# Seventy-two of eighty early expert blocks as unsplit fp32 products, and twenty-eight of their results held in SBUF

## The chip, the core and the metric

The kernel runs on one core of one Trainium2 chip. The metric is the device time of one execution in microseconds (us). The engines are TensorE (PE in the rows, PEld for its weight loads), VectorE (DVE), ScalarE (ACT), GpSimd (POOL) and SyncE (SP, which only issues copies here).

## What is computed

One decoder layer over 512 tokens of width 1024 in fp32. Three groups of attention heads and an output projection come first. Then comes a feed-forward part in which each token has 8 heads, and each head retrieves 16 of 16384 one-neuron experts:

```python
    cand = (v1[..., :, None] + v2[..., None, :])            # scores of two half keys
    top_s, pos = lax.top_k(cand, PEER_TOPK)
    expert = jnp.take_along_axis(cand_idx, pos, axis=-1)
    gate = jax.nn.softmax(top_s, axis=-1)
    a = jnp.einsum('cd,ced->ce', x_c, u[e_c])               # h . u of each chosen expert
    w = jax.nn.gelu(a, approximate=False) * g_c
    return jnp.einsum('ce,ced->cd', w, v[e_c])              # sum of w * v
```

The attention is outside of this study. All of the change lies in the expert part.

## The kernel before, in words

**Two ways through the experts.** For the first 128 tokens (chunk `GC`) the kernel gathers the rows that were chosen: 128 gathers of rows of `u`, each followed by a dot product on VectorE (`dot`, L494), a gelu, and 128 gathers of rows of `v`, each added up on VectorE (L505). For the next 64 tokens it gathers rows of `u` alone, 64 times, with the same `dot`. For the last 320 tokens (`TD`) it computes the product of the tokens with **all** rows of `u`, in 128 blocks of 128 experts (`a_block`). For all 384 tokens outside `GC` the product with `v` runs over all 128 blocks too (`w_block`), with a weight that is zero where an expert wasn't chosen.

**A block's first product.** `u_parts` (L529) loads 512 KB of `uT` into one of three buffers `flat`. Where the block is split, ScalarE writes a rounded copy `hi` (L91), VectorE the remainder `lo` (L92), both into `yT`, and the buffer `flat` is free again. `a_block` (L539) then issues three products for each of eight slices (`mm3`, L100 to L102), 24 in all, on operands of type fp32r. Where the block is whole (L527), nothing is split. `flat` itself is the weight of eight plain fp32 products with `hF` (L544), and stays occupied until they are done. `hF` is a sum that GpSimd makes once (L608). A gelu on ScalarE (L551) moves the result out of PSUM into `ag`, of which two can be under way in PSUM (tag `t`).

**Early and late blocks.** Blocks 0 to 79 (`NSP`) are early: their first products run while routing and scatter are still going on. The result of most is written to DRAM (`ad`, L658) and read back before the second product (`agr`, L684). The last `KEEP` of them stay in SBUF instead (`kept`, L548), in a pool `kp` that is opened at L651. Blocks 80 to 127 are late. Their first products alternate with the second products of all 128 blocks.

**Routing and scatter.** VectorE picks experts and gates (`top16`, `route`). Then `scatter` (L615) makes the table of weights: for every four tokens a one-hot tile `o1` (L621), four gated one-hot tiles `o2` (L625), four products on TensorE (L628) and a copy on ScalarE (L629) into `stage`. Eight such units fill one `stage`, which goes to DRAM (`gd`, L633). There are 96 units. Those of the 64 tokens (`iX`) need the dots of these tokens (L642 to L648). The second products need the finished table (`gt`, L688) and the PSUM banks that scatter has used.

**What sets the order.** The program is recorded, and a scheduler then fixes one order of instructions for each engine. On the chip every engine works through its own list. Gathers go through four buffers `row`, one queue of GpSimd. All other copies are issued by SP in one list. Rows of `u` for `GC` are one step for each early block (L659 to L661), and the rest follows where the scheduler puts it. The pool `rp` with routing's tiles was open to the end.

The numbers that choose which blocks are whole and which are kept:

```python
KEEP = 8
WHOLE = 48
    def whole(b):
        return WHOLE <= b < NSP and b % 2 == 1
```

Of the kernel before, what the change touches and what calls it, by code (L numbers as in the profile page):

```python
# [37 lines left out]
NSP = 80  # L38
# [6 lines left out]
SCB = 4  # L45
EM = 4
GR = 1.0
KEEP = 8
WHOLE = 48
HX = P // 2  # L50
DX = DC[0]
T0 = DX * P + HX
# [8 lines left out]
def layer_kernel(ctx, tc, x, xT, memT, mem, w_in, w_kv, w_out, w_q, cols, qk_gain, g_bc, subT, bias_tab,  # L61
# [4 lines left out]
    def tile_pool(**kw):  # L66
        return tc.tile_pool(reuse_waits="tile", **kw)
# [6 lines left out]
    hd = dram.tile([HX, D], F32, name="hd")  # L74
    ad = [dram.tile([P, TD], F32, name=f"ad{b}") for b in range(NSP - KEEP)]

# [21 lines left out]
    def mm3(o, a, b, start, stop):  # L98
        (ah, al), (bh, bl) = a, b
        T.matmul(o, ah, bh, start=start, stop=False)  # L100
        T.matmul(o, ah, bl, start=False, stop=False)  # L101
        T.matmul(o, al, bh, start=False, stop=stop)  # L102
# [17 lines left out]
    def bank(tag=None):  # L120
        if tag is None:
            tag = CYC[turn[0] % len(CYC)]
            turn[0] += 1
        return pps.tile([P, S], F32, tag=tag, name=tag, bufs=BANKS[tag])

    def quarters(t):
        return t.rearrange("p (a b) -> p a b", b=P)
# [225 lines left out]
    def w_piece(n, k2):  # L353
        raw = flat().rearrange("p (m k d) -> p m k d", m=4, d=P)
        DMA.dma_start(raw, w_q[4 * n:4 * n + 4, :, 2 * k2:2 * k2 + 2, :].rearrange("m p k d -> p m k d"))
        hi, lo = (qp.tile([P, 4, 2, P], F32R, tag=t_, name=t_, bufs=WB) for t_ in ("hi", "lo"))
        split(hi, lo, raw, V if n == 0 and k2 % 2 == 0 else G)
        w_pieces[n, k2] = (hi, lo)
# [48 lines left out]
    def top16(n, src, vals, idx, pool, tag):  # L407
        rest = [pool.tile([P, n], F32, tag=f"{tag}{q % 4}", name=f"{tag}{q % 4}", bufs=1) for q in range(len(src))]
        for q, s_ in enumerate(src):
            V.max(vals[q][:, 0:8], s_)  # L410
        for q, s_ in enumerate(src):
            V.max_index(idx[q][:, 0:8], vals[q][:, 0:8], s_)
        for q, s_ in enumerate(src):
            V.match_replace(rest[q], vals[q][:, 0:8], s_, -3e38)
        for q in range(len(src)):
            V.max(vals[q][:, 8:16], rest[q])
        for q in range(len(src)):
            V.max_index(idx[q][:, 8:16], vals[q][:, 8:16], rest[q])
# [105 lines left out]
    halves, last_lo, kept = {}, [], {}  # L524

    def whole(b):
        return WHOLE <= b < NSP and b % 2 == 1  # L527

    def u_parts(b, i, e_lo):  # L529
        ur = flat().rearrange("p (k e) -> p k e", e=NK)  # L530
        DMA.dma_start(ur, uT[b])
        if whole(b):
            halves[b] = [ur]
            return
        halves[b] = [t.rearrange("p k t -> p (k t)")[:, i * D:(i + 1) * D].rearrange("p (k e) -> p k e", e=NK)
                     for t in yT]
        last_lo.append(split(*halves[b], ur, e_lo))

    def a_block(b):  # L539
        us = halves.pop(b)  # L540
        ap = bank("t")[:, :TD]
        for k in range(KD):
            if whole(b):
                T.matmul(ap, us[0][:, k, :], hF[:, k, :], start=k == 0, stop=k == KD - 1)  # L544
            else:
                mm3(ap, [t[:, k, :] for t in us], [t[:, k, T0:] for t in hT], k == 0, k == KD - 1)
        if NSP - KEEP <= b < NSP:
            ag = kept[b] = kp.tile([P, TD], F32, name=f"kept{b}")  # L548
        else:
            ag = ub.tile([P, TD], F32, tag="ag", name="ag", bufs=3)  # L550
        A.activation(ag, ap, AF.Gelu)  # L551
        return ag

    with tile_pool(name="qa", bufs=1) as qa, tile_pool(name="qp", bufs=2) as qp:
        mix_out([GC] + DC, yT, rg, hT, "l")
        G.memset(ga[0], 0.0)
        rp = ctx.enter_context(tile_pool(name="rp", bufs=1, side="right"))
        hx = rp.tile([P, D], F32, name="hx")
        for i in range(2):
            DMA.dma_start(hx[i * HX:(i + 1) * HX, :], hd)  # L560
        exp_x = rp.tile([P, HX], I32, name="exp_x")
        avx = rp.tile([P, HX], F32, name="avx")
        gx, ax = (rp.tile([P, NSLOT], F32, name=n_) for n_ in ("gx", "ax"))
        sub = qa.tile([P, 2 * PH, NK], F32, name="sub", bufs=1)
        for n in range(4):
            for k2 in range(KD // 2):
                if (n, k2) not in w_pieces:
                    w_piece(n, k2)
            if n == 0:
                DMA.dma_start(sub, subT)  # L570
            w = [w_pieces[n, k2] for k2 in range(KD // 2)]
            acc = quarters(bank("s"))
            for k in range(KD):
                mm3(acc, [t[:, k, GC * P:(GC + 1) * P] for t in hT], [t[:, :, k % 2, :] for t in w[k // 2]],
                    k == 0, k == KD - 1)
            qy = qa.tile([P, 4, P], F32, tag="qyg", name="qyg", bufs=1)
            A.activation(qy, acc, AF.Copy)
            tr = quarters(bank("o"))
            for i in range(4):
                T.transpose(tr[:, i, :], qy[:, i, :], ident)  # L580
            qt = qa.tile([P, 4, P], F32, tag="qt", name="qt", bufs=1)
            A.activation(qt, tr, AF.Copy)
            sc = quarters(bank("o"))
            for i in range(4):
                T.matmul(sc[:, i, :], qt[:, i, :], sub[:, 4 * n + i, :], start=True, stop=True)
            sx = qa.tile([P, 4, P], F32, tag="sx", name="sx", bufs=SCB)
            A.activation(sx, sc, AF.Copy)
            top16(NK, [sx[:, i, :] for i in range(4)], [tv[GC][i % 2][:, 2 * n + i // 2, :] for i in range(4)],
                  [ti[GC][i % 2][:, 2 * n + i // 2, :] for i in range(4)], qp, "r")
            route(GC, q0=2 * n, nq=2)  # L590
            for i in range(4):
                m = 4 * n + i
                acc = bank("s")[:, :TQ]
                for k in range(KD):
                    mm3(acc, [t[:, i, k % 2, :] for t in w[k // 2]], [t[:, k, S - TQ:] for t in hT],
                        k == 0, k == KD - 1)
                qy = qp.tile([P, TQ], F32, tag="qy", name="qy")
                A.activation(qy, acc, AF.Copy)
                sc = quarters(bank("o"))[:, 0:len(DC), :]
                for j in range(len(DC)):  # L600
                    T.matmul(sc[:, j, :], qy[:, j * P:(j + 1) * P], sub[:, m, :], start=True, stop=True)
                sx = qa.tile([P, 4, P], F32, tag="sx", name="sx", bufs=SCB)[:, 0:len(DC), :]
                A.activation(sx, sc, AF.Copy)
                top16(NK, [sx[:, j, :] for j in range(len(DC))], [tv[c][m % 2][:, m // 2, :] for c in DC],
                      [ti[c][m % 2][:, m // 2, :] for c in DC], qp, "r")
# [5 lines left out]
    with tile_pool(name="oh", bufs=2) as oh:  # L611
# [3 lines left out]
        def scatter(c, iT, q, col, dots):  # L615
            stage = oh.tile([P, NK, GT], F32, tag="stage", name="stage")
            for t4 in range(0, GT, 4):
                t0 = col + t4
                o1 = oh.tile([P, 4, NK], F32, tag="o1", name="o1", bufs=3)
                o2 = oh.tile([P, 4, NK], F32, tag="o2", name="o2", bufs=3)  # L620
                V.tensor_tensor(o1, iT[:, 0, t0:t0 + 4, None].to_broadcast([P, 4, NK]),  # L621
                                iota[:, None, :].to_broadcast([P, 4, NK]), ALU.is_equal)
                for j in range(4):
                    i2, gate = (iT[:, i, t0 + j:t0 + j + 1] for i in (1, 2))
                    V.tensor_scalar(o2[:, j, :], iota, i2, gate, ALU.is_equal, ALU.mult)  # L625
                gp = quarters(bank("s"))
                for j in range(4):
                    T.matmul(gp[:, j, :], o1[:, j, :], o2[:, j, :], start=True, stop=True)  # L628
                A.activation(stage[:, :, t4:t4 + 4].rearrange("p e t -> p t e"), gp, AF.Copy)  # L629
                s_ = next(early, None) if dots else None  # L630
                if s_ is not None:
                    dot(s_, hx, avx, exp_x)
            DMA.dma_start(gd[(c - DX) * (P // GT) + q], stage)  # L633
# [14 lines left out]
        A.activation(iX[:, 2, :], tp[:, 0, 0:HX], AF.Copy)  # L648
        for q in range(HX // GT):
            scatter(DX, iX, q, q * GT, False)  # L650
    kp = ctx.enter_context(tile_pool(name="kp", bufs=1))  # L651
    for b in range(NSP):
        while loaded < min(b + 4, NSP):
            u_parts(loaded, loaded % 4, V)
# [9 lines left out]
    with tile_pool(name="vb", bufs=2) as vb:  # L664
        acc = [[bank("ssssoo"[2 * c + n]) for n in range(2)] for c in range(len(DC))]
        inl, spl = (list(range(r0, r1, NB)) for r0, r1 in ((NSP, NK), (0, NSP)))
        starts, a, b = [], 0, 0
# [123 lines left out]
```

## Time and profile before

| | us |
|---|---|
| three executions | 1654.09, 1656.85, 1657.8 |
| their median | 1656.85 |
| the profiled execution | 1650.69 |
| its span, first to last instruction | 1648.9 |
| busy in it: PE / DVE / ACT / POOL | 1528.8 / 1348.3 / 669.9 / 560.0 |
| mean granted clock of TensorE | 0.959 of full |

The profile is of one execution. Times inside it count from the first instruction. A busy share is a mean over stages with different limits, so the tables by stage below are of more use than the totals. A matmul's own duration overlaps its neighbour's, so what one costs in a row of matmuls is the distance between two starts.

### The profile page before, as it was taken

The page shows a single profiled execution, that of the slowest core. Times are in us where ns is not written, and L with a number is a line of the kernel's source. Part 1 is how long each engine was busy: PE and PEld are TensorE (multiplying, and loading weights), DVE is VectorE, ACT ScalarE, POOL GpSimd, SP SyncE. Part 2 cuts the span into 40 slices and gives each one's busy share as a digit, 9 for nine tenths or more (in the row PEclk, how much of TensorE's full clock was granted, in tenths as well). Part 3 has the DMA queues.
Part 4 walks back from the last instruction along what each step waited for, and adds up shares of the span by engine and source line. Part 5 has one row for each costly group of instructions (what it writes and reads, how often), then busy time and mean ns, then how long its engine had stood idle before and what let it go on. Part 6 is the DMA issues. An engine that isn't in the chain of part 4 may idle for free.

```text
span 1648.9 us, 23114 instructions
## 1 busy us (share of the span) xinstructions
PE 1528.8 (93%) x7918; PEld 1318.3 (80%) x7918; DVE 1348.3 (82%) x3096; ACT 669.9 (41%) x1149; POOL 560.0 (34%) x403
## 2 busy tenths in 40 slices
PE   8999989898999878899866799999999999999998
PEld 6887658897999767688766688888888888888886
DVE  6666755599999999999998588787888788787886
ACT  7444643333443433334533243434443433434332
POOL 5320013234205454543334443333333323332350
PEclk9999999998999999999956999999999999999999
DMA  8312025123356678889987999999998999999986
GB/s 325 103 52 109 1 79 185 62 78 103 118 180 240 238 260 319 292 302 368 330 309 266 368 344 323 368 329 323 362 326 304 354 325 344 345 313 349 330 295 236
DMA packets 176292, 422.83 MB, mean 256 GB/s; under 512 B 14192, under 2 KB 90992, under 8 KB 173488
## 3 DMA queue, kind: packets, MB, share of 16 engines
q1 hardware_dynamic: 130096, 253.58, 44.0%
q0 software_dynamic: 46080, 167.79, 28.0%
q8 instruction: 62, 1.02, 0.2%
q14 instruction: 54, 0.44, 0.1%
HBM read 379.87 MB, written 41.42 MB: 255 GB/s over the span
## 4 chain that ended last, share of the span: by engine, by line
PE 62%; DVE 27%; DMA 5%; issue 3%; ACT 2%; POOL 1%; ACTq 0%; DVEq 0%; SPq 0%; POOLq 0%
PE s L100 9%; PE s L101 9%; PE s L102 9%; PE t L100 5%; DVE row L494 5%; PE t L101 5%; PE t L102 5%; PE o L100 4%; PE o L101 4%; PE o L102 4%; DVE o L625 4%; DVE yT L92 3%; DVE o L621 3%; PE o L335 2%; DMA flat<-uT 2%
## 5 line engine op out<-in xcount | busy, mean ns | idle before, releaser
L102 PE MATMUL t<-hT,yT 128*128 128x320 f32 x896 | 285.5, 320 | 31.0 <-DVE yT L92 30.9
L100 PE MATMUL t<-hT,yT 128*128 128x320 f32 x896 | 288.7, 322 | 14.4 <-ACT ag L551 12.4
L101 PE MATMUL t<-hT,yT 128*128 128x320 f32 x896 | 284.4, 317 | 0.0
L488 POOL DMA_INDIRECT row<-v,exp_g x128 | 155.0, 1211 | 288.6 <-DVE ga L505 268.0
L488 POOL DMA_INDIRECT row<-u,exp_g x128 | 161.6, 1263 | 258.9 <-DVE row L494 247.6
L102 PEld LDWEIGHTS t<-hT,yT 128*128 128x128 f32 x896 | 174.2, 195 | 38.4 <-DVE yT L92 34.0
L101 PE MATMUL s<-yT,ws 128*128 128x512 f32 x512 | 202.2, 396 | 0.0
L91 ACT ACTIVATE ws<-w 128x384 fp32r<-128x384 f32 x128 | 67.1, 525 | 320.4 <-PE o L101 285.0
L102 PE MATMUL s<-yT,ws 128*128 128x512 f32 x512 | 196.3, 396 | 0.0
L100 PEld LDWEIGHTS t<-hT,yT 128*128 128x128 f32 x896 | 174.6, 195 | 23.8 <-ACT ag L551 16.0
L91 ACT ACTIVATE yT<-flat 128x1024 fp32r<-128x1024 f32 x112 | 118.5, 1058 | 171.2 <-DMA flat<-uT 85.8
L92 DVE TENSOR_TENSOR yT<-vr,yT 128x1024 fp32r<-128x1024 f32 x128 | 156.4, 1222 | 32.6 <-ACT yT L91 32.4
L101 PEld LDWEIGHTS t<-hT,yT 128*128 128x128 f32 x896 | 174.6, 195 | 5.1
L494 DVE SCALAR_TENSOR_TENSOR row<-row,hg 128x1024 f32<-128x1024 f32 x128 | 154.3, 1220 | 21.1 <-DMA row<-u,exp_g 21.0
L505 DVE SCALAR_TENSOR_TENSOR ga<-row,gw,ga 128x1024 f32<-128x1024 f32 x128 | 163.8, 1279 | 1.8 <-DMA row<-v,exp_g 1.3
L92 DVE TENSOR_TENSOR yT<-flat,yT 128x1024 fp32r<-128x1024 f32 x112 | 147.1, 1322 | 19.7 <-ACT yT L91 16.3
L91 ACT ACTIVATE yT<-vr 128x1024 fp32r<-128x1024 f32 x128 | 134.2, 1048 | 51.5 <-PE o L102 44.8
L628 PE MATMUL s<-o,o 128*128 128x128 f32 x768 | 124.0, 316 | 31.3 <-DVE o L625 31.3
L100 PE MATMUL s<-yT,ws 128*128 128x512 f32 x512 | 151.9, 394 | 0.0
L628 PEld LDWEIGHTS s<-o,o 128*128 128x128 f32 x768 | 115.6, 225 | 40.6 <-issue 23.7
L629 ACT ACTIVATE stage<-s 128x512 f32<-128x512 f32 x96 | 101.0, 1092 | 107.9 <-PE s L628 107.4
L92 DVE TENSOR_TENSOR ws<-w,ws 128x384 fp32r<-128x384 f32 x128 | 70.9, 557 | 81.6 <-ACT ws L91 73.4
(284 smaller groups left out, 3145.7 us busy)
## 6 DMA issues: line engine op xcount, KB each, us to landing
flat<-uT SPq DMA_DIRECT2D x128, 512.0 KB
vr<-v SPq DMA_DIRECT2D x128, 512.0 KB
gd<-stage SPq DMA_DIRECT2D x12, 2048.0 KB
gt<-gd SPq DMA_DIRECT2D x32, 768.0 KB
ad<-ag SPq DMA_DIRECT2D x72, 160.0 KB
agr<-ad SPq DMA_DIRECT2D x72, 160.0 KB
wraw<-w_in SPq DMA_DIRECT2D x8, 1024.0 KB
flat<-w_q SPq DMA_DIRECT2D x16, 512.0 KB
```

Source lines behind the costliest of these rows:

```text
L91: A.activation(hi, src, AF.Copy)
L92: return (e_lo or V).tensor_sub(lo, src, hi.bitcast(F32))
L100: T.matmul(o, ah, bh, start=start, stop=False)
L101: T.matmul(o, ah, bl, start=False, stop=False)
L102: T.matmul(o, al, bh, start=False, stop=stop)
L488: G.indirect_dma_start(out=row, out_offset=None, in_=table, in_offset=bass.IndirectOffsetOnAxis(ap=ids[:, s_:s_ + 1], axis=0))
L494: V.scalar_tensor_tensor(row, row, 1.0, h, ALU.mult, ALU.mult, accum_out=to[:, s_:s_ + 1])
L505: V.scalar_tensor_tensor(ga[0], row, gw[:, s_:s_ + 1], ga[0], ALU.mult, ALU.add)
L621: V.tensor_tensor(o1, iT[:, 0, t0:t0 + 4, None].to_broadcast([P, 4, NK]), iota[:, None, :].to_broadcast([P, 4, NK]), ALU.is_equal)
L625: V.tensor_scalar(o2[:, j, :], iota, i2, gate, ALU.is_equal, ALU.mult)
L628: T.matmul(gp[:, j, :], o1[:, j, :], o2[:, j, :], start=True, stop=True)
L629: A.activation(stage[:, :, t4:t4 + 4].rearrange("p e t -> p t e"), gp, AF.Copy)
```

## The change

Blocks 8 to 79 are all whole, odd and even; before, it was the 16 odd ones from 49 on. That makes 72 whole blocks in the place of 16. Routing's pool `rp` is closed after the scatter, and the pool of kept results is opened where `rp` was. 28 results are kept (blocks 52 to 79) in the place of 8 (72 to 79), and 52 go through DRAM in the place of 72.

```diff
-KEEP = 8
-WHOLE = 48
+KEEP = 28
+WHOLE = 8
@@
     def whole(b):
-        return WHOLE <= b < NSP and b % 2 == 1
+        return WHOLE <= b < NSP
@@
-        rp = ctx.enter_context(tile_pool(name="rp", bufs=1, side="right"))
+        rp_scope = ctx.enter_context(ExitStack())
+        rp = rp_scope.enter_context(tile_pool(name="rp", bufs=1, side="right"))
@@
             scatter(DX, iX, q, q * GT, False)
-    kp = ctx.enter_context(tile_pool(name="kp", bufs=1))
+    rp_scope.close()
+    kp = ctx.enter_context(tile_pool(name="kp", bufs=1, side="right"))
```

Lines after L556 stand one further down in the changed kernel, those after L650 two. The scheduler orders the changed program anew. Three places of its lists follow.

VectorE, from the last units of scatter to the first weight of a second product, before (`row,av<-row,hg` is a dot, `yT<-flat` the split of a first product's block, `yT<-vr` of a second one's):

```order
L494 SCALAR_TENSOR_TENSOR row,av<-row,hg 128x1024 x2
L621 TENSOR_TENSOR o_6355<-iX,iota 128x512
L625 TENSOR_SCALAR o_6356<-iota,iX 128x128 x4
L494 SCALAR_TENSOR_TENSOR row,av<-row,hg 128x1024 x9
L92 TENSOR_TENSOR yT_1451<-flat,yT_1450 128x1024
L92 TENSOR_TENSOR yT_1451<-vr,yT_1450 128x1024
L494 SCALAR_TENSOR_TENSOR row,av<-row,hg 128x1024 x4
L92 TENSOR_TENSOR yT_1451<-vr,yT_1450 128x1024
L92 TENSOR_TENSOR yT_1451<-flat,yT_1450 128x1024 x2
L494 SCALAR_TENSOR_TENSOR row,av<-row,hg 128x1024 x2
L698 TENSOR_TENSOR w<-ag,gt 128x320
```

The same place in the changed kernel:

```order
L494 SCALAR_TENSOR_TENSOR row,av<-row,hg 128x1024 x2
L622 TENSOR_TENSOR o_6335<-iX,iota 128x512
L626 TENSOR_SCALAR o_6336<-iota,iX 128x128 x4
L494 SCALAR_TENSOR_TENSOR row,av<-row,hg 128x1024 x9
L92 TENSOR_TENSOR yT_1431<-vr,yT_1430 128x1024 x2
L494 SCALAR_TENSOR_TENSOR row,av<-row,hg 128x1024 x47
L92 TENSOR_TENSOR yT_1431<-flat,yT_1430 128x1024
L494 SCALAR_TENSOR_TENSOR row,av<-row,hg 128x1024
L92 TENSOR_TENSOR yT_1431<-flat,yT_1430 128x1024
L494 SCALAR_TENSOR_TENSOR row,av<-row,hg 128x1024 x2
L700 TENSOR_TENSOR w<-ag,gt 128x320
```

Before, 13 dots stand ahead of the split of block 80 (the first of the pair `yT<-flat ... x2`); now 56 stand ahead of it (the first `yT<-flat`).

TensorE, the end of scatter and what follows, in the changed kernel (`s<-o,o` is one unit of scatter, eight rows `t<-hF,flat` are one whole block, the L100 to L102 that follow are block 80):

```order
L629 MATMUL s<-o_6323,o_6322 128x128 x4
L629 MATMUL s<-o_6336,o_6335 128x128 x4
L544 MATMUL t<-hF,flat 128x320 x208
L100 MATMUL t<-hT_2638,yT_1430 128x320
L101 MATMUL t<-hT_2639,yT_1430 128x320
L102 MATMUL t<-hT_2638,yT_1431 128x320
```

26 whole blocks (54 to 79) stand between scatter's last unit and block 80. Before, it was six, three split and three whole (74 to 79).

SP's list from the last scatter tables on, before:

```order
L633 DMA gd<-stage 128x4096 x4
L688 DMA gt<-gd 128x12x128
L692 DMA vr<-v 128x1024 x3
L688 DMA gt<-gd 128x12x128
L684 DMA agr<-ad_69 128x320
L684 DMA agr<-ad_70 128x320
L684 DMA agr<-ad_71 128x320
L531 DMA flat<-uT 128x1024 x2
L692 DMA vr<-v 128x1024
L531 DMA flat<-uT 128x1024
```

and in the changed kernel:

```order
L634 DMA gd<-stage 128x4096 x5
L690 DMA gt<-gd 128x12x128
L694 DMA vr<-v 128x1024 x3
L690 DMA gt<-gd 128x12x128
L686 DMA agr<-ad_69 128x320
L686 DMA agr<-ad_70 128x320
L686 DMA agr<-ad_71 128x320
L531 DMA flat<-uT 128x1024 x2
L694 DMA vr<-v 128x1024 x2
L531 DMA flat<-uT 128x1024 x28
```

The `x28` are the loads of blocks 59 to 86, and the pair ahead of them those of blocks 57 and 58. Before, the load that stands first behind the tables was that of block 79.

## Rows read from the trace of the kernel before

**Rows 1.** The page's first line.
```profile
span 1648.9 us, 23114 instructions
```

**Rows 2.** Stages: from:to, length, PE, PEld, DVE, ACT, POOL busy; PEclk, DMA, GB/s.
```profile
320.00:446.00 126.00, 118.47 (x716) 114.53 (x715) 126.00 (x652) 49.73 (x77) 51.41 (x21) 0.96 0.31 96
446.00:527.00 81.00, 74.46 (x477) 72.88 (x476) 79.33 (x314) 32.99 (x47) 18.66 (x9) 0.95 0.58 185
527.00:774.00 247.00, 208.03 (x1260) 188.78 (x1259) 241.21 (x491) 97.19 (x125) 115.13 (x75) 0.94 0.81 296
774.00:897.00 123.00, 93.44 (x503) 84.17 (x502) 121.09 (x304) 54.17 (x57) 47.18 (x40) 0.74 0.85 306
897.00:938.00 41.00, 30.47 (x128) 24.66 (x127) 19.53 (x30) 8.00 (x14) 16.95 (x13) 0.82 1.00 379
938.00:1644.00 706.00, 705.80 (x3455) 601.33 (x3453) 568.69 (x712) 275.22 (x477) 244.11 (x198) 1.00 0.92 328
```

**Rows 3.** Chain that ended last, 855 to 945 us: start, us, what.
```profile
859.14 1.14 DVE row L494 x2
860.28 0.60 DVE o L621
860.88 1.03 DVE o L625 x4
...
923.28 7.48 DMA flat<-uT
930.89 6.88 PE t L544 x16
```

**Rows 4.** Timeline of VectorE behind the last unit of scatter: start, us, what [idle before].
```profile
896.37 1.22 DVE L494 SCALAR_TENSOR_TENSOR row<-row,hg 128x1024 f32<-128x1024 f32 x1
...
901.15 1.23 DVE L494 SCALAR_TENSOR_TENSOR row<-row,hg 128x1024 f32<-128x1024 f32 x1 [0.98 <-DMA row<-u,exp_g]
910.31 1.23 DVE L494 SCALAR_TENSOR_TENSOR row<-row,hg 128x1024 f32<-128x1024 f32 x1 [7.92 <-DMA row<-u,exp_g]
...
920.88 1.22 DVE L494 SCALAR_TENSOR_TENSOR row<-row,hg 128x1024 f32<-128x1024 f32 x1 [5.57 <-DMA row<-u,exp_g]
922.03 1.22 DVE L92 TENSOR_TENSOR yT<-flat,yT 128x1024 fp32r<-128x1024 f32 x1
923.17 1.22 DVE L92 TENSOR_TENSOR yT<-vr,yT 128x1024 fp32r<-128x1024 f32 x1
```

**Rows 5.** Groups of instructions by line: busy us, mean ns | idle before.
```profile
L92 DVE TENSOR_TENSOR yT<-flat,yT 128x1024 fp32r<-128x1024 f32 x112 | 147.1, 1322 | 19.7 <-ACT yT L91 16.3 <-PE t L102 2.6 <-issue 0.8
```

**Rows 6.** Timeline of TensorE around 897 us: start, us, what.
```profile
891.91 1.22 PE L628 MATMUL s<-o,o 128*128 128x128 f32 x8 [0.65 <-DVE o L625]
...
899.99 0.47 PE L102 MATMUL t<-hT,yT 128*128 128x320 f32 x1
...
900.25 0.47 PE L100 MATMUL t<-hT,yT 128*128 128x320 f32 x1
...
905.43 4.47 PE L544 MATMUL t<-hF,flat 128*128 128x320 f32 x16
...
910.03 0.31 PE L102 MATMUL t<-hT,yT 128*128 128x320 f32 x1
...
910.18 0.30 PE L100 MATMUL t<-hT,yT 128*128 128x320 f32 x1
```

**Rows 7.** GpSimd's copy queue (packets, MB, share of 16 engines) and a block's load.
```profile
q0 software_dynamic: 46080, 167.79, 28.0%
...
flat<-uT SPq DMA_DIRECT2D x128, 512.0 KB
```

**Rows 8.** Timeline of SP behind scatter's last table: start, us, issue.
```profile
910.60 2.24 SPq L692 DMA_DIRECT2D vr<-v  x3
...
924.41 0.33 SPq L692 DMA_DIRECT2D vr<-v  x1
```

## Prediction

> **What bounds the kernel now.** The span is 1648.9 us [rows 1], and the execution it belongs to took 1650.69, so 1.8 us lie around it. The median of the runs is 1656.85, 0.4% more. I make the sum against the profiled execution and add its difference to the median. About 0.2% (3 us) is what a measurement here can tell from no change.
>
> I read the busy time by stage first, because it shows that the limit changes three times [rows 2]. From 320 to 897 us VectorE sets the pace: it is busy in 567.6 of 577 us, with the splits of the early blocks, routing, scatter and dots. From 897 to 938 it is busy for only half the time, TensorE waits too, and the copy engines are busy throughout (share 1.00, 379 GB/s). I call this stretch the gap: scatter is over, the last early blocks are not. From 938 on TensorE is busy in 705.8 of 706 us at full clock. Nothing that VectorE or the copies do there shows in the time.
>
> So the end is set by one moment, the start of block 80 at 938: all products behind it are the same 48 late blocks and 128 second products in both kernels. What the change does to the time is what it does to that moment. It moves in two steps: scatter ends earlier or later than 896.4, and the gap is shorter or longer than 41 us.
>
> **What the change removes before the end of scatter.** 56 blocks are no longer split. 63 splits stood ahead of scatter's last unit in VectorE's list, 8 stand there now: 55 fewer. In a row of such instructions one starts 1.14 us after the other (922.03 and 923.17) [rows 4], which makes 63 us. The mean of the group is 1.32 [rows 5], since a few are stretched; by that it is 73. I take 68, between them. 96 dots stand ahead of the last unit in the place of 105; a dot takes 1.14 [rows 3], so 10 us more. VectorE had only 9.4 us of idle time in these 577, so nearly all of the 78 us would show. ScalarE loses its half of the splits too, but it is busy for less than half of each of these stages [rows 2]; I cost that at nothing. The 20 results that no longer go to DRAM and back save 3.3 MB each way, on copies that are not the limit before 897 (share 0.81 to 0.85) or after 938. That is nothing for the time, as long as TensorE sets the pace of the last stage.
>
> **What it adds before the end of scatter.** A whole block takes 4.47 us from its first start to its last end [rows 6]. Records outlast the start of the next by 0.16 there (0.31 long, 0.15 apart), so 4.3 a block in a row. A split block is 24 products 0.147 apart, 3.5 us at full clock. Each changed block costs TensorE 0.8 more. In the stretch from the first dots to the scatter of the last 64 tokens the new list holds 33 whole blocks (142 us) and 61 scatter units of 1.22 (74): 216 us. VectorE's list there holds 67 dots (77), 61 units of 0.60 + 1.03 (99), and routing, for which the old stage leaves some 40 us after its dots, units and splits are taken out of 241. That is 216 too. Before, TensorE was busy in 208 of 247 us there, beside 241 of VectorE. Now neither has slack, and units wait for blocks on TensorE's list, blocks for their load (a `flat` is now held until its products are done, so loads run three ahead and no more), and VectorE for the units. The copy of `avx` that VectorE needs next stands behind the load of block 55 in SP's list, and that load behind block 52 on TensorE. No row shows this coupling. Its cost lies between 0 and some 35 us (the slack of 39 that TensorE had). I take 10, nearer the lower end, because three units are buffered. **Scatter then ends 68 us earlier, at 828.**
>
> **What it adds behind scatter.** Giving routing's pool back does not let the kept blocks run beside scatter: ScalarE's list has all remaining copies of scatter ahead of the first kept gelu, and only two first products fit in PSUM. So 26 whole blocks stand behind scatter where six stood, and 56 dots stand ahead of block 80's split on VectorE where 13 stood. Three prices for this new gap:
>
> - Copies. The old gap moved 41 us x 379 GB/s = 15.5 MB [rows 2]. To it come 43 gathers of 167.79 / 320 = 0.524 MB [rows 7], 22.5 MB, and 22 more loads of 0.524 MB, 11.5 MB. 49.5 MB at 379 GB/s are 131 us; at the 328 of the last stage, 151.
> - TensorE. 26 x 4.3 = 112 us if it never waits. It will wait: the loads from block 59 on stand behind a pair of `vr` on SP, whose buffers come free with the splits of `vr`. The first of these ran 27 us after scatter (896.4 to 923.17) [rows 4], and the next `vr` went out right after it [rows 8]. A load then takes up to 7.48 to land [rows 3]. Blocks 54 to 56 run in that time, and 23 x 4.3 = 99 us follow: 126 to 133.
> - Gathers. The most that any stage shows is 40 in 123 us (POOL) [rows 2], 3.1 each, with VectorE as the limit; at that pace 56 dots take 174 us. With VectorE free I expect the copies to set it.
>
> I take the copies at 365 GB/s, between the two rates and nearer to that of the gap, whose mix it is: 136 us. The clock costs little. At half clock products are 0.26 apart [rows 6], and by 910.03 they are 0.15 apart; in the new gap this falls into the wait.
>
> **The sum.** Scatter ends 68 us earlier, the gap grows from 41 to 136: +95 - 68 = +27 us. Block 80 starts at about 965, the span is 1676, and on the median 1656.85 + 27 = **1684 us**.
>
> A rule that bears on the gap: the Trainium skill, "DMA: Bandwidth & Descriptors", section "Where 436 GB/s comes from", gives 435 GB/s as the ceiling of the ports and about 358 as one core's share of HBM. The trace's 379 lies above the second, so for a single busy core that isn't a limit. By 358 the gap would be 138 us, by 435 an estimated 114.
>
> **The rivals.**
>
> 1. *Faster: the gap is no longer than its products.* If the blocks behind scatter start at once and never wait, the gap is 112 + 3 = 115 us. With the full saving (73 + 10, no coupling) that is +74 - 83 = -9: 1648. The change wins once the gap stays under 41 plus the saving, 109 to 124. For it speaks that TensorE alone needs 112. Against it: 49.5 MB in 115 us are 430 GB/s where the busiest stretch shows 379, and SP's order holds the loads back. The skill's ceiling of 435, named above, would just allow it. Chance 0.10, and 0.07 for an end within 0.2% between this and my forecast.
> 2. *The saving isn't there.* In the stretch of scatter TensorE becomes the bound, with 35 us of waiting; then 43 us are saved and the time is 1656.85 + 95 - 43 = 1709. The busy sums above (216 against 216) speak for it; the buffering speaks against. Or the 24 splits that leave routing's end were filling waits there, with the same outcome. Chance 0.13.
> 3. *Gathers are as slow as in every stage shown,* 3.1 us each. The gap is 174, +133 - 68 = +65: 1722. For it speaks that four buffers `row` limit how many are under way, against it that VectorE or full copies explain the pace wherever it shows. Chance 0.10.
> 4. *My forecast,* +10 to +50: chance 0.60.
>
> That the change doesn't do what it says is partly so already: the pool is returned early, but the lists use it only behind scatter.
>
> **How the numbers follow.** Slower by over 0.2%: 0.60 + 0.13 + 0.10 = 0.83. Same 0.07, faster 0.10. The range reaches from just under the old median, leaving out most of rival 1, to 1715, which takes in rival 2 and leaves out the middle of rival 3: 1655 to 1715.
>
> **What would show it right or wrong.** Right: in the new profile VectorE's last one-hot tile stands near 828 us (before: 896.4); then some 136 us with copies near 1.00, 26 whole blocks, and dots with idle time before them put down to gathers; then 706 us of unbroken TensorE. Wrong in its first step if scatter ends after 850, with TensorE full and VectorE waiting for products. Wrong in its second if the gap is under 120, or if TensorE's blocks there wait for nothing. Wrong as a whole if the last stage isn't 706 us again.

## The result and the profile after

| | before | after |
|---|---|---|
| median of four executions each, us | 1655.47 | 1688.92 |
| their range | 1651.69 to 1657.8 | 1687.62 to 1692.19 |
| the profiled execution | 1650.69 | 1689.36 |
| its span | 1648.9 | 1687.6 |
| scatter ends (VectorE's last one-hot tile) | 896.4 | 840.5 |
| block 80 starts | 937.4 | 975.6 |

The changed kernel is slower: ratio 1.0221, interval 1.0202 to 1.024. The forecast was 1684 us, that is +27; the medians differ by 33.5, the two profiled executions by 38.7. Scatter ends 56 us earlier, and block 80 starts 38 us later all the same.

The changed kernel by stages follows (columns as in [rows 2]). The last two rows answer to the gap and the last stage there.

```profile
503.00:735.00 232.00, 210.21 (x1015) 160.79 (x1016) 215.73 (x481) 76.21 (x97) 102.63 (x75) 0.97 0.87 308
735.00:840.50 105.50, 69.72 (x329) 62.30 (x328) 101.08 (x262) 42.48 (x43) 41.96 (x34) 0.67 0.75 273
840.50:975.60 135.10, 118.36 (x422) 82.86 (x422) 72.22 (x117) 15.93 (x33) 69.58 (x57) 0.91 0.99 367
975.60:1682.00 706.40, 706.20 (x3457) 601.77 (x3456) 529.81 (x642) 275.97 (x477) 212.33 (x164) 1.00 0.85 298
```

The gap has grown from 41 to 135.1 us. In it TensorE is busy for most of the time, and the copies have a share of 0.99. The last stage is what it was: TensorE is busy in 706.2 of 706.4 us. The four pieces of the 38.7 us between the spans are then: 3.0 from before the expert part (VectorE's first MAX8 of routing starts at 317.43, before at 314.47, ahead of the first load of any block, at 381 and 378), -58.9 from there to scatter's end, +94.1 in the gap, and +0.5 behind it (712.0 from block 80 to the end, before 711.5).

TensorE's timeline in the gap (start, us, what, idle before it):

```profile
839.92 2.05 PE L629 MATMUL s<-o,o 128*128 128x128 f32 x8 [2.69 <-DVE o L626]
843.38 15.68 PE L544 MATMUL t<-hF,flat 128*128 128x320 f32 x48 [1.41 <-ACT kept L551]
874.39 101.65 PE L544 MATMUL t<-hF,flat 128*128 128x320 f32 x368 [15.33 <-DMA flat<-uT]
975.64 0.55 PE L100 MATMUL t<-hT,yT 128*128 128x320 f32 x1
```

Three blocks run as soon as the kept gelu can go. One wait of 15.33 us for a load follows, then 23 blocks of 4.4 us without a pause, and block 80 right behind them. The chain of waits tells where the 15.33 come from (start, us, what):

```profile
842.00 1.06 ACT stage L630
843.06 0.03 ACT kept L551
843.09 9.25 DMA gd<-stage
...
853.01 1.02 SPq L694
...
855.03 1.18 SPq L690
...
856.25 9.04 SPq L686
...
866.35 7.90 DMA flat<-uT
...
874.39 97.36 PE t L544 x352
```

The last table has to land before its first reader is issued. Behind that reader, SP's list holds three `vr` (L694), the next `gt` (L690) and three `agr` (L686), the first of which is held for 9 us. Only then comes the next `flat`. The second row shows something else: the first kept gelu runs right after ScalarE's last copy of scatter.

### The profile page after: what moved, and what is told of

The parts are those of the page before. It is cut to its first block, busy times and chain, and to the rows that moved or that the text cites. A ratio compares the mean times of both kernels' runs of the same rounds, so it can differ in the third digit from the quotient of the medians.

```text
span 1687.6 us, 21992 instructions
## 1 busy us (share of the span) xinstructions
PE 1571.3 (93%) x7470; PEld 1287.2 (76%) x7470; DVE 1292.1 (77%) x3040; ACT 619.7 (37%) x1093; POOL 551.8 (33%) x403
## 4 chain that ended last, share of the span: by engine, by line
PE 62%; DVE 24%; DMA 7%; issue 3%; ACT 1%; POOL 1%; SPq 1%; DVEq 0%; POOLq 0%; ACTq 0%
PE s L100 9%; PE s L102 9%; PE s L101 9%; PE t L544 6%; PE o L100 4%; PE o L101 4%; PE o L102 4%; DVE row L494 4%; PE t L100 4%; PE t L102 4%; PE t L101 4%; DVE o L626 4%; DMA row<-u,exp_x 3%; DVE o L622 2%; PE o L335 2%
## 5 line engine op out<-in xcount | busy, mean ns | idle before, releaser
L544 PE MATMUL t<-hF,flat 128*128 128x320 f32 x1152 | 327.9, 443 | 24.5 <-DMA flat<-uT 15.3
L544 PEld LDWEIGHTS t<-hF,flat 128*128 128x128 f32 x1152 | 221.4, 195 | 115.1 <-issue 22.8
L488 POOL DMA_INDIRECT row<-v,exp_g x128 | 170.9, 1335 | 278.4 <-DVE ga L505 260.7
L488 POOL DMA_INDIRECT row<-u,exp_g x128 | 155.9, 1218 | 203.3 <-DVE row L494 183.2
L102 PE MATMUL s<-yT,ws 128*128 128x512 f32 x512 | 196.1, 396 | 0.0
L629 PE MATMUL s<-o,o 128*128 128x128 f32 x768 | 130.1, 329 | 55.1 <-DVE o L626 53.6
L629 PEld LDWEIGHTS s<-o,o 128*128 128x128 f32 x768 | 120.0, 234 | 71.8 <-issue 45.0
L100 PE MATMUL s<-yT,ws 128*128 128x512 f32 x512 | 152.0, 394 | 0.0
L100 PE MATMUL t<-hT,yT 128*128 128x320 f32 x448 | 138.5, 309 | 0.0
L102 PE MATMUL t<-hT,yT 128*128 128x320 f32 x448 | 138.3, 309 | 0.2 <-DVE yT L92 0.2
L101 PE MATMUL t<-hT,yT 128*128 128x320 f32 x448 | 138.2, 309 | 0.0
L488 POOL DMA_INDIRECT row<-u,exp_x x64 | 85.5, 1336 | 130.3 <-DVE row L494 102.5
L101 PEld LDWEIGHTS s<-yT,ws 128*128 128x128 f32 x512 | 96.4, 188 | 20.1
L102 PEld LDWEIGHTS s<-yT,ws 128*128 128x128 f32 x512 | 96.1, 188 | 19.9
```

Of the source, the lines that this page charges most:

```text
L488: G.indirect_dma_start(out=row, out_offset=None, in_=table, in_offset=bass.IndirectOffsetOnAxis(ap=ids[:, s_:s_ + 1], axis=0))
```

## The experiments

My theory was that the two parts of the change work against each other: unsplit blocks save time, and the kept results put 14 more blocks behind scatter, because their pool reaches into memory that scatter still uses. By the sizes in the program, the tiles of routing's pool take some 24,400 bytes per partition beside scatter's pool. A result takes 1280, so 19 fit. The runs came in three batches, in which the medians of before were 1653.92 (unsplit part alone, kept part alone, 19 kept, half of the products), 1651.10 (20 kept, two pools, 72 and 76 early blocks) and 1654.72 (68 early blocks, three buffers). Each ratio is against the runs of its own batch; differences between medians of different batches are good to some 4 us.

**1. The unsplit part alone.**

```diff
-KEEP = 28
+KEEP = 8
-        rp_scope = ctx.enter_context(ExitStack())
-        rp = rp_scope.enter_context(tile_pool(name="rp", bufs=1, side="right"))
+        rp = ctx.enter_context(tile_pool(name="rp", bufs=1, side="right"))
-    rp_scope.close()
-    kp = ctx.enter_context(tile_pool(name="kp", bufs=1, side="right"))
+    kp = ctx.enter_context(tile_pool(name="kp", bufs=1))
```

> Only the unsplit part of the change: blocks 8 to 79 whole, 8 results kept, routing's pool open to the end. In its lists 12 blocks (68 to 79) stand behind scatter where 26 stand in the changed kernel, 91 dots ahead of scatter's last unit, 25 ahead of block 80's split. Theory A (the kept results, whose memory reaches into that of scatter, push 14 blocks behind scatter, and this alone makes the change slow): scatter's last one-hot tile ends at 845 to 860, the gap to block 80 falls from 135 us to 60 to 75, block 80 starts at 910 to 930, and the last stage is again 712: 1625 to 1645 us, faster than both kernels. Theory B (whole blocks beside scatter make TensorE the limit there): scatter ends at 890 to 905, with VectorE waiting for products, the gap is 65, and the time is 1670 to 1685, slower than before.

Measured: 1622.2 us, ratio 0.9817 (0.9794 to 0.9839). Theory A, and a little better than it said: scatter ends 12 us ahead of its range. The stages from scatter's end to block 80 and behind it, then TensorE's timeline in the first of them:

```profile
833.40:907.90 74.50, 61.39 (x219) 42.57 (x218) 33.95 (x54) 10.89 (x19) 28.20 (x25) 0.89 1.00 379
907.90:1615.00 707.10, 706.35 (x3458) 601.84 (x3456) 571.29 (x717) 275.06 (x477) 261.01 (x200) 1.00 0.93 328
```

```profile
837.65 9.86 PE L544 MATMUL t<-hF,flat 128*128 128x320 f32 x36
853.12 14.85 PE L544 MATMUL t<-hF,flat 128*128 128x320 f32 x48 [5.62 <-DMA flat<-uT]
875.47 32.84 PE L544 MATMUL t<-hF,flat 128*128 128x320 f32 x112 [7.50 <-DMA flat<-uT]
907.91 0.55 PE L100 MATMUL t<-hT,yT 128*128 128x320 f32 x1
```

Scatter ends at 833.4, and the gap is 74.5 us with about half of the blocks. This part of the change is a gain of 32 us.

**2. The kept part alone.**

```diff
-WHOLE = 8
+WHOLE = 48
-        return WHOLE <= b < NSP
+        return WHOLE <= b < NSP and b % 2 == 1
```

> Only the kept part of the change: 28 results kept in the place of routing's pool, blocks split as before. In its lists 26 blocks stand behind scatter as in the changed kernel, half of them split; 53 splits and 104 dots stand ahead of scatter's last unit, nearly as before. Theory A (the kept part makes the change slow): scatter ends at about 885, the gap is 115 to 130, block 80 starts at 1000 to 1015, the time is 1710 to 1725 us, slower than the changed kernel. Theory B (whole blocks make it slow): scatter ends at 885 to 897 and split blocks fill the gap faster, 60 to 80 us, so block 80 starts at 945 to 975 and the time is 1655 to 1690, at or below the changed kernel.

Measured: 1727.19 us, ratio 1.0449 (1.0425 to 1.0474): a loss of 73 us, 2 us above the range of theory A. The gap in the profile:

```profile
887.10:1012.50 125.40, 110.56 (x527) 90.16 (x526) 67.64 (x101) 27.27 (x46) 55.40 (x44) 0.94 0.92 333
```

It is 125.4 us long although half of its blocks are split and cost TensorE less. So the kept part makes the change slow, and the unsplit part hides some of that. The two alone (-32 and +73) add up to +41 where both together give +33.

**3. Nineteen results kept, and twenty.** These two differ by one number, and by one tile that does or does not reach into scatter's pool.

```diff
-KEEP = 28
+KEEP = 19
```

> The changed kernel with 19 results kept in the place of 28. 19 of them (24.4 KB per partition) fit into what routing's pool gives back, without scatter's pool. In its lists 12 blocks (68 to 79) stand behind scatter where 26 stood. Theory A (what counts is whether the kept results reach into scatter's memory): as without the kept part: scatter ends at 845 to 860, the gap is 60 to 75, the time 1625 to 1645 us. Theory B (the cost of the kept part grows with each result that is kept, 20 more of them costing about 95 us of gap): 11 more than before cost some 52 us of gap, 93 in all; with scatter at 845 to 860 block 80 starts at 938 to 953, and the time is 1651 to 1667.

```diff
-KEEP = 28
+KEEP = 20
```

> The changed kernel with 20 results kept, one more than fits into what routing's pool gives back, so that the pool reaches into scatter's memory by one tile. In its lists 18 blocks (62 to 79) stand behind scatter, with 43 dots ahead of block 80's split on VectorE; with 19 kept it was 12 blocks. Theory A (what counts is whether the pool reaches into scatter's memory): six more blocks of 4.4 us behind scatter, and so 24 to 28 us more than with 19 kept: 1643 to 1651 us. Theory B (the cost grows with the number of results kept, 66 us for the nine from 19 to 28): one more costs 7 us, 1625 to 1631.

Measured: 1620.86 us with 19, ratio 0.9799 (0.978 to 0.9819); 1650.31 with 20, ratio 0.9984 (0.997 to 0.9998). Theory A both times, with 19 a little better than it said. One more result costs 29 us. What ScalarE shows of the kept results, with 19 and then with 20 (duration min/median/max in ns, first and last start in us):

```profile
L551 ACT ACTIVATE kept<-t x19: 419/437/465, 803.6 to 911.1; 128x320 f32<-128x320 f32 x19
```

```profile
L551 ACT ACTIVATE kept<-t x20: 418/437/460, 839.5 to 938.2; 128x320 f32<-128x320 f32 x20
```

With 19 the first is written at 803.6, while scatter is still going on (it ends at 836.8). With 20 it is written at 839.5, just behind scatter's end at 837.2. TensorE then has 18 blocks to do in the gap:

```profile
840.01 15.59 PE L544 MATMUL t<-hF,flat 128*128 128x320 f32 x48 [1.41 <-ACT kept L551]
871.02 67.11 PE L544 MATMUL t<-hF,flat 128*128 128x320 f32 x240 [15.42 <-DMA flat<-uT]
937.72 0.55 PE L100 MATMUL t<-hT,yT 128*128 128x320 f32 x1
```

This is the changed kernel's pattern, with 15 blocks behind the wait where it has 23. What counts is the step from 19 to 20, where the pool reaches into scatter's memory. The number kept doesn't explain it: experiment 4 keeps all 28.

**4. All 28 kept, in two places.** The same results stay in SBUF, but only the last nine lie in scatter's memory.

```diff
-            ag = kept[b] = kp.tile([P, TD], F32, name=f"kept{b}")
+            ag = kept[b] = (kp if b < NSP - KEEP + 19 else kp2).tile([P, TD], F32, name=f"kept{b}")
     kp = ctx.enter_context(tile_pool(name="kp", bufs=1, side="right"))
+    kp2 = ctx.enter_context(tile_pool(name="kp2", bufs=1))
```

> The changed kernel with all 28 results kept, but in two pools: blocks 52 to 70 in what routing gives back (19 tiles), blocks 71 to 79 in scatter's memory. In its lists 11 blocks (69 to 79) stand behind scatter where 26 stand in the changed kernel. Theory A (the place of the first kept results made the change slow, not their number): scatter ends at 835 to 845, the gap is 65 to 76 us, and the time is 1612 to 1626 us, as with 19 kept. Theory B (keeping 28 results is itself what costs): 1670 to 1690, as the changed kernel.

Measured: 1623.41 us, ratio 0.9826 (0.9807 to 0.9846): theory A, with scatter's end (846.3) and the gap (64.4) each about 1 us outside its ranges. Its kept results on ScalarE, and then the same row of the changed kernel:

```profile
L551 ACT ACTIVATE kept<-t x28: 420/438/483, 745.1 to 911.1; 128x320 f32<-128x320 f32 x28
```

```profile
L551 ACT ACTIVATE kept<-t x28: 420/437/463, 842.9 to 976.1; 128x320 f32<-128x320 f32 x28
```

Two lines of code take 65 us off the changed kernel. Keeping results neither costs nor gains anything that these runs tell apart: 8, 19 and 28 of them give 1622.2, 1620.86 and 1623.41, with intervals that overlap. Handing the 28 tiles of the one pool out in reverse was not run; so whether the first writer waits for its own tile's memory or for that of the pool as a whole stays open.

**5. What sets the length of the gap.** Blocks 54 to 79 with every other product:

```diff
-        for k in range(KD):
+        ks = [k for k in range(KD) if not 54 <= b < NSP or k % 2 == 0]
+        for k in ks:
-                T.matmul(ap, us[0][:, k, :], hF[:, k, :], start=k == 0, stop=k == KD - 1)
+                T.matmul(ap, us[0][:, k, :], hF[:, k, :], start=k == 0, stop=k == ks[-1])
```

> The changed kernel with four of the eight products left out in each of blocks 54 to 79 (half of the contraction of the first product isn't computed there); loads, gathers and dots are all there. A block takes TensorE 2.2 us in the place of 4.4. Theory A (TensorE, behind SP's list, sets the gap of 135 us, and dots with their gathers end just beside it: the 56th dot came 130 us behind scatter): the gap falls only by what lies between the two, to 122 to 131 us, and the time is 1676 to 1686 us. Theory B (TensorE sets the gap with nothing close behind): 23 blocks save 50 us, the gap is 85 us, the time 1639. Theory C (the copies set it, TensorE's unbroken row is a coincidence): nothing changes, the gap is 133 to 137 us and the time 1686 to 1692. The copies' rate tells the last from the first: 49.5 MB need 131 us at 379 GB/s.

Measured: 1661.7 us, ratio 1.0056 (1.0035 to 1.0077). That is 27 us less than the changed kernel, between theories A and B. The gap and then TensorE in a piece of it:

```profile
836.60:949.40 112.80, 71.02 (x215) 44.66 (x214) 56.01 (x90) 16.35 (x34) 51.66 (x45) 0.82 1.00 383
```

```profile
870.57 9.75 PE L545 MATMUL t<-hF,flat 128*128 128x320 f32 x24 [22.86 <-DMA flat<-uT]
882.26 8.39 PE L545 MATMUL t<-hF,flat 128*128 128x320 f32 x24 [1.94 <-DMA flat<-uT]
```

TensorE now waits for load after load, and the copies are full: share 1.00, 383 GB/s. So theory B falls: the copies stand close behind. Theory A was right in kind and missed the size, because the scheduler reordered this kernel too: 44 dots stand in the gap in the place of 57, and 13 gathers (6.8 MB) went out of it with them. So the shorter gap by itself doesn't refute theory C. 112.8 us x 383 are 43.2 MB, and the changed kernel moved 135.1 x 367 = 49.6 MB; at 383 those would take an estimated 130 us. By that estimate 17 of the 22 us are the bytes that left, and 5 are the products.

What speaks against theory C is a row of the changed kernel, SP's waits from 870 to 976 us (in total, times, longest):

```profile
SPq L531 <- PE t L544: 88.9, 22, 7.0
```

Its loads waited 22 times for products, whose buffers they need, while TensorE's 23 blocks waited for no load. In the changed kernel TensorE thus set the end of the gap, and the copies alone would have needed an estimated 5 us less.

**6. Fewer early blocks.** What is left of the gap with 19 results kept is whole blocks of 4.4 us. As late blocks they are split and cost TensorE 3.53.

```diff
-NSP = 80
+NSP = 72
-KEEP = 28
+KEEP = 19
```

> With 19 results kept, and 72 early blocks in the place of 80: blocks 72 to 79 are now late, split (24 products, 3.53 us each) in the place of whole (4.4 us each). In its lists three blocks (69 to 71) stand behind scatter, then two late ones, and then the second products, which need the tables. Theory A (what is left of the gap is blocks on TensorE and the wait for tables): the second products start at 866 to 875 where they start at about 915 with 80 early blocks, and the stage behind them grows by 8 x 3.53 = 28 us: 1600 to 1610 us, 0.7 to 1.3% under the kernel with 19 kept. Theory B (VectorE or the copies, which have 8 more splits and some 15 more gathers in the last stage, become its limit): TensorE is no longer unbroken there, 1615 to 1640.

The same with 76, and with 68:

> As the kernel before it, with 76 early blocks: 7 blocks (69 to 75) behind scatter, of 4.4 us each, and a wait of 13 us as with 80. Theory A: the second products start at 885 to 892, the last stage grows by 4 x 3.53 = 14 us: 1602 to 1613 us, between 72 and 80 early blocks. Theory B (last stage limited by VectorE or the copies with more of the work moved there): 1615 to 1635.

> With 19 results kept and 68 early blocks in the place of 72: four more late blocks. In its lists three blocks (65 to 67) stand behind scatter, as with 72, so that the wait for the tables isn't shortened. Theory A (the last stage begins when the tables are there, and TensorE is unbroken from then on): the stage grows by 4 x 3.53 = 14 us and starts no earlier: 1620 to 1628 us, slower than with 72. Theory B (fewer early blocks also free the stretch of scatter, which ends earlier by the copies and products that it loses): scatter ends at 835 or before, and the time is 1608 to 1615.

Measured: 72 early blocks 1611.29 us, ratio 0.9756 (0.9739 to 0.9774); 76 of them 1619.44, ratio 0.9808 (0.9786 to 0.9829); 68 of them 1635.08, ratio 0.9875 (0.984 to 0.9911). TensorE between scatter and the second products, with 72 and then with 68:

```profile
848.24 12.55 PE L544 MATMUL t<-hF,flat 128*128 128x320 f32 x46
864.45 0.42 PE L100 MATMUL t<-hT,yT 128*128 128x320 f32 x1 [3.66 <-ACT yT L91]
...
868.77 0.64 PE L102 MATMUL t<-hT,yT 128*128 128x320 f32 x1 [3.77 <-DVE yT L92]
```

```profile
872.92 0.64 PE L102 MATMUL t<-hT,yT 128*128 128x320 f32 x1 [5.95 <-DVE yT L92]
```

With 72 the first late block starts at 864.45, 46 us before that of the kernel with 80 (910.63), and from there to the end it takes 745.6 us in the place of 713.3. Behind the two waits shown TensorE is unbroken, as theory A had it. That nets 14 us in the profiles, 10 in the medians and 7 by the two ratios. It beats both kernels: 2.4% under before. The time missed its range by 1 us, with the two waits of 3.66 and 3.77 in it.

With 68 the first late block starts no earlier (866.28), and the time from there grows to 764.2, 19 more where 14 were forecast. Theory A held in kind, and the time missed its range by 7 us; TensorE was not unbroken, but waited 7.3 us for splits (5.95 of them in the row above). Theory B falls: scatter ended at 848.5.

76 gives no gain over 80 that these runs tell apart, and missed its range: TensorE waited three times for loads (8.7 us) ahead of the first late block at 890.45, and the rest took 727.0 us, as much longer than with 80 as forecast (14).

**7. Three buffers for gathered rows.** This is about the waits of VectorE in the stretch of scatter.

```diff
-    gr = ctx.enter_context(tile_pool(name="gr", bufs=4, side="right"))
+    gr = ctx.enter_context(tile_pool(name="gr", bufs=3, side="right"))
```

(to the kernel with 19 results kept)

> The kernel with 19 results kept, with three buffers for gathered rows in the place of four. It tells what VectorE waits for in the 21 us that it is idle in the stretch of scatter, where its dots wait for gathers. Its lists have 81 dots ahead of scatter's last unit where 91 stood, which by itself is 11 us less of VectorE's work there. Theory A (the number of buffers limits how many gathers are under way): the idle time ahead of dots grows by a third or more, from 21 to 35 us or more, and eats the 11 us. Theory B (the gathers share the copies with everything else, whose share is 0.87 there, and four or three under way makes little difference): idle time stays at 15 to 25 us, and scatter ends about 10 us earlier, at 825 to 830. The time of the whole is put at 1615 to 1650 under both, since the gathers left over for the gap come more slowly too.

Measured: 1662.55 us, ratio 1.0032 (1.0013 to 1.0052). What VectorE waited for until scatter's end at 852.3 (us in total, times, longest):

```profile
DVE row L494 <- DMA row<-u,exp_x: 24.4, 12, 5.5
DVE row L494 <- DMA row<-u,exp_g: 12.8, 5, 4.5
```

37.2 us where it is 21 with four buffers. From the first MAX8 of routing to scatter's end it took 522.1 us (518.2 with four), with ten dots fewer on the list. Theory A. The time as a whole missed its range: routing started 12 us later here, at 330.2, the gap took 80 us, 7 more, and block 80 to the end 729 us, 15 more, with a chain that ends in gathers of `v`. Why routing started later I did not follow.

## Why the prediction was right, step by step

**The saving before scatter's end** was put at 68 us and is 58.9, from the first MAX8 of routing on. That is the term that was mis-sized. In the two profiled executions it is 9.1 of the 11.7 us by which +27 fell short of 38.7; 3.0 lie ahead of the expert part, and the gap and the last stage make up for 0.4. That the medians come within 5 us of the forecast is in part luck. Summed by distance between starts, with idle time taken apart, VectorE's list there changed as follows: the 55 splits -74.1, the dots -11.7, idle time +11.4, and other instructions +15.6.

- *The splits* took 74.1 by the distance between starts, close to my higher price of 73: 55 at 1.14 are 62.7, and seven that were long add 11.7, each of them beside an instruction of GpSimd. That part did not go away: with the splits gone other instructions are long beside GpSimd in their place (the rows are in the last section). Added up over the stretch, VectorE's long instructions exceed the usual length of their kind by some 34 us before and 33 after. If all of the +15.6 is put down to that, the splits were worth 58.5, under both of my prices. Most of it is additions and one-hot tiles that ran beside GpSimd; that all of it is, isn't shown.
- *The dots* were put at 10 and are 11.7.
- *The coupling* was put at 10 and is 11.4 us of additional idle time, but the mechanism was the wrong one. I had VectorE wait for TensorE's products. It waited for gathers. Waits of VectorE in the changed kernel, from 500 us to scatter's end:

```profile
DVE row L494 <- DMA row<-u,exp_x: 16.3, 8, 6.1
DVE row L494 <- DMA row<-u,exp_g: 4.4, 3, 2.1
```

and in the kernel before, from 527 us on:

```profile
DVE row L494 <- DMA row<-u,exp_x: 2.5, 3, 1.2
DVE o L621 <- PE s L628: 2.2, 1, 2.2
DVE row L494 <- DMA row<-u,exp_g: 1.9, 2, 1.2
```

Without splits between them, dots come due sooner than four buffers can deliver rows. Experiment 7 bears that out.

**The gap** was put at 136 us and is 135.1. The bytes were right: 49.5 MB forecast, 49.6 moved. I took the copies as what sets it; by SP's waits, shown with experiment 5, TensorE set it, with the copies an estimated 5 us behind. So the number was luck in part: my price by way of TensorE was 126 to 133 us (27 until loads go out, 7.5 to land, 99 for 23 blocks), and the two prices lay close together. Measured: 25.9, 7.9 and 101.3, since a block in a row took 4.40 and not 4.3. The sign that I gave for a wrong second step came half true: after one wait of 15.33 us, 23 blocks waited for nothing. What holds the loads back is not the splits of `vr` that I named, but the landing of the last table and the first `agr` behind it in SP's list. What held that `agr` for 9 us the trace doesn't say.

**The kept blocks don't run beside scatter:** right, read from the lists. I did not ask why, and so did not see that it hung on the size of the pool: 19 tiles would have fitted, and one more is enough to push the kept blocks behind scatter. That was to be read from the sizes of the pools.

**The rivals.** A gap of 115 us would have needed 430 GB/s; the fullest stretches here, in four kernels, show 367 to 383. Of the two ceilings that the prediction took from the Trainium skill ("DMA: Bandwidth & Descriptors", section "Where 436 GB/s comes from"), the lower one (358) is exceeded in all of them, and the upper one (435) is reached in none. The second rival (saving lost, 43 us left) did not come. TensorE did come close, as the sum of 216 against 216 had it: from 503 to 735 us it is busy in 210.21 of 232, beside 215.73 of VectorE. But all of VectorE's waits there are for gathers (the 16.3 us above), none for a product. From 735 on VectorE kept the bound, with 101.08 of 105.5 us where TensorE has 69.72. The third rival took gathers at 3.1 us each: 57 of them in 135.1 us are 2.4 each.

**The last stage** was unchanged, as forecast, in this kernel and wherever 80 blocks were early and four buffers were there: 711 to 714 us.

## What to carry to other kernels

Count in tiles what a pool given back early holds, and what else still lies behind it. In these kernels one tile that reached into memory in use put the first writer behind its last reader, and everything behind that writer in the engines' lists as well; two pools in the place of one cost two lines. When work is taken off the engine that sets the pace, ask what the next stage has to do before it can start, and move into that stage what its engine does more cheaply.

## What the runs showed of the hardware

**Some instructions of VectorE last until GpSimd's end, where they meet.** In the kernel before, GpSimd's sum `hF` and the split that met it:

```profile
440.43 5.76 POOL L608 TENSOR_TENSOR hF<-hT,hT 128x2560 f32<-128x2560 f32 x1
```

```profile
441.60 5.67 DVE L92 TENSOR_TENSOR yT<-flat,yT 128x1024 fp32r<-128x1024 f32 x1
```

In the changed kernel no split stands there. An addition of 64 columns is caught in its place, which elsewhere takes 0.2 us, and later one-hot tiles beside another pair on GpSimd:

```profile
442.41 5.65 POOL L609 TENSOR_TENSOR hF<-hT,hT 128x2560 f32<-128x2560 f32 x1
...
615.82 3.43 POOL L449 TENSOR_TENSOR eq<-eq,ci 128x800 f32<-128x800 f32 x2
```

```profile
442.71 5.43 DVE L436 TENSOR_TENSOR cv<-tv,tv 128x64 f32<-128x64 f32 x1
...
615.52 4.58 DVE L626 TENSOR_SCALAR o<-iota,iT 128x128 f32<-128x128 f32 x4
```

The addition ends when GpSimd's sum does (448.1 both), the first of the four one-hot tiles at 619.3, where GpSimd's pair ends at 619.25, the split 1.1 us behind the sum. Four such one-hot tiles take 1.1 us elsewhere. Not every instruction is caught: a TENSOR_REDUCE that began at 440.70 in the kernel before, beside the same sum, took its usual 0.97 us. So a group's mean (1322 ns for a split [rows 5], 1219 in the changed kernel) holds time that does not go away with the group. The Trainium skill, "Trainium Architecture — The Big Picture", section "What this means for kernel authors", says that the two engines share a pair of ports under an exclusive lock, not a split of bandwidth. The trace agrees for the instructions that were caught: the addition of 0.2 us took 5.43, until GpSimd's sum ended.

**The clock in the last stretch of scatter.** From 735 us to scatter's end the changed kernel was granted 0.67 of TensorE's full clock, with TensorE busy in 69.7 of 105.5 us. The kernel of experiment 1, whose blocks run beside scatter there, was granted 1.00 from 735 to 833 with 93.4 of 98 us. TensorE's clock rose again only within the first three blocks of the gap (granted 0.50, the lower of its two levels, from 843.4 to 848, and 1.00, the upper one, from 852.6 on): they took 15.68 us, where three blocks take 13.2 at 4.4 each. It cost nothing, since the wait for loads came behind them.
